# Channel mixing of a two-layer decoder trunk: all eleven pairs' early products ahead, the first operands of the downward product split before the stage border, modulation sums closed by columns

## Chip, cores and metric

The kernel runs on one core of a Trainium2 chip. The metric is the device time of one execution in microseconds (us); the median of three runs counts. One profiled execution gives the trace: PE is TensorE's matrix multiply, PEld its weight loads, DVE is VectorE, ACT ScalarE, POOL GpSimd, and SP the engine that issues nearly all DMAs, in the order of its own queue.

## What is computed

Two layers, a sequence of 1024 positions, width 1024, all float32. The part that the change touches:

```python
def reference(...):
    c_act = silu(c)
    for l in range(2):
        mod = c_act @ ada_w[l] + ada_b[l]              # 6 x 1024 modulation values
        shift_m, scale_m, gate_m, shift_f, scale_f, gate_f = split(mod, 6)
        h = rms_norm(x, g_pre_mix[l]) * (1 + scale_m) + shift_m
        ...                                            # attention beside a pooling mixer, output projection
        x = x + gate_m * rms_norm(mix, g_post_mix[l])
        h = rms_norm(x, g_pre_ffn[l]) * (1 + scale_f) + shift_f
        f = (silu(h @ w_gate[l]) * (h @ w_up[l])) @ w_down[l]     # inner width 2816
        x = x + gate_f * rms_norm(f, g_post_ffn[l])
```

## The kernel before

**Precision.** A float32 operand is split into a high part (ACT, line 213) and the rest (DVE, line 214, one subtraction), and a product is three matmuls: high by high (line 239), high by low (242), low by high (243). A split of 128x1024 is one instruction on ACT and one on DVE.

**Upward product.** The sequence is two halves of 512 positions, the inner width eleven pairs of two 128-blocks. Both products of the channel mixing use a scheme with seven block products in place of eight. For the upward product five of a pair's seven (right operands T2, T3, T1, B22, T4) need sums over both halves; two (right operands B11 and B21) need the first half alone and are the *early products*. `up_firsts` makes these for some pairs while the second half is still being normed: `FIRST = (3, 6)` says three pairs beside the attention's end and six after the output projection. Each pair there is two jobs of 24 matmuls; it stores its sums (`firsts`) and the gated result (`a11`) to DRAM. The six are interleaved with `second_norm`: four steps of the post norm, then four steps `k` (one for each 128 rows of a half) in which `up_sums` builds T1 to T4 and B22 with `split`s and sums on ACT, DVE and POOL (lines 972 to 980). `run(stream, steps, (other, n))` paces the other stream: it takes n steps of the other over `steps` steps of the stream; here 12 over 12. Then `up_pair` goes through the eleven pairs: those with early products load them back and make five products, the last two make all seven. A pair's weights stand in two `raw` tiles (two buffers); lines 1076 to 1082 form sums of weights on DVE, a `split` follows, then the matmuls.

**Downward product.** `down` makes seven products p1, p2, p5, p6, p3, p7, p4 of 11 units each (12 matmuls a unit), in groups of one, then two units. `left_of` loads a left operand from DRAM and splits it; right operands from w_down are split into tiles `bh` and `ph` or `bl`. `bh` lies in the memory of the region "down", which takes the place of the region "up" (tiles T1 to T4, B22); each tile waits until what lay there has been used. B11's rows of w_down, six transfers with 2.75 MB in all, go into the `hT` tiles, which hold the first half's B11 and B21 until the last early product has read them: `load(B11, g)` stands in the last pair's second step.

**Modulation sums.** `ada_sum` sums eight weight tiles `ar` (two buffers) times a value each on DVE (lines 271 and 273) into an `ada` tile of 128x512; summing that over partitions gives 512 values. For layer 1's first norm four such sums run beside layer 0's downward product (`ada_pair`): each is split (ACT, DVE), two matmuls against a column of ones pick it into one row of a bank (367, 368), and after the fourth the rows are copied by ACT, turned by four transposes (375) and added to the biases (379). The stream has 20 steps, and is paced 60 over 77, so that it is through after 26 units.

The order of an engine's instructions is made by a scheduler from this program, and it may put an instruction well ahead of its place in the text.

Of the kernel before, what the change touches and what calls it, by code (L numbers as in the profile page):

```python
# [12 lines left out]
F32R = mybir.dt.float32r  # L13
# [7 lines left out]
P = 128  # L21
# [44 lines left out]
def hybrid_decoder_kernel(  # L66
# [70 lines left out]
    def msc_bank():  # L137
        return ps.tile([P, 512], F32, tag="msc", name="msc", bufs=3)
# [72 lines left out]
    def split(hi, lo, src):  # L211

        nc.scalar.activation(hi, src, AF.Copy)  # L213
        nc.vector.tensor_sub(lo, src, hi.bitcast(F32))  # L214
# [44 lines left out]

    def ada_sum(l, n0, got):  # L260

        src = ada_w[l].rearrange("(p j) n -> p j n", j=KD)
        acc, ws = None, []
        for j in range(0, KD + 2, 2):
            for i, w in enumerate(ws, j - 2):
                if i == 0:
                    acc = t_("ada", [P, 512])  # L270
                    nc.vector.tensor_scalar(acc, w, c_act[:, 0:1], None, op0=ALU.mult)
                else:
                    nc.vector.scalar_tensor_tensor(  # L273
                        acc, w, c_act[:, i : i + 1], acc, op0=ALU.mult, op1=ALU.add
                    )
            ws = []
            if j < KD:
                for i in (j, j + 1):
                    w = t_("ar", [P, 512])
                    nc.sync.dma_start(w, src[:, i, n0 : n0 + 512])  # L280
                    ws.append(w)
                yield
        got += [t_("ph", [P, 512], F32R), t_("ph", [P, 512], F32R)]
        split(*got, acc)
        yield
# [73 lines left out]
    def ada_pair(l, sub, cols, ab):  # L359
# [28 lines left out]
        ]  # L388

    gates = {}  # L390

# [30 lines left out]
    def ada_stream(jobs):  # L422

        for l, n0, close in jobs:
            got = []
            yield from ada_sum(l, n0, got)
            close(*got)
# [698 lines left out]

    def down(l, wd, load, kept, fn, ended, last):

# [45 lines left out]

        def left_of(a, p0, p1, c0, c1):

            n, w = p1 - p0, c1 - c0
            raw, lh, ll = (
                part(tag, 2 * w).rearrange("p (i n) -> p i n", n=w)[:, :n, :] for tag in ("raw", "hi", "lo")
            )  # L1180
            nc.sync.dma_start(raw, kept[a][:, p0:p1, c0:c1])
            split(lh, ll, raw)
            return lh, ll

        def products(name, g, lh, ll, rights, banks, ts, evict):
# [17 lines left out]
        for name, a, right, evict in jobs[:-1]:  # L1203
            banks = [acc_bank() for _ in range(NT)]
            for g, (p0, p1) in enumerate(DOWN_GROUPS):
                n = p1 - p0
                lh, ll = left_of(a, p0, p1, 0, T)
                src = right(g)
                rights = []
                for i in range(n):  # L1210
                    rights.append((t_("bh", [P, 512], F32R), t_("ph" if count[0] % 5 < 3 else "bl", [P, 512], F32R)))
                    count[0] += 1
                    split(*rights[i], src[:, i, :])
# [12 lines left out]
        for ts in ((0, 1), (2, 3)) if last else (range(NT),):  # L1226
            banks = {t: acc_bank() for t in ts}
            for g, (p0, p1) in enumerate(DOWN_GROUPS):
                n = p1 - p0
                lh, ll = left_of(a, p0, p1, ts[0] * P, (ts[-1] + 1) * P)  # L1230
                if len(kept4) == g:
# [79 lines left out]

    FIRST = (3, 6)
    for l in range(DEPTH):
# [85 lines left out]
        if l + 1 < DEPTH:  # L1399
            nxt = layer_cols(l + 1)  # L1400
            jobs = ada_pair(l + 1, 0, nxt["cols"], nxt["abm"])
        side = ada_stream(ada_gate(l, 1))
# [14 lines left out]
        side = ada_stream(jobs)  # L1417

        region("down")
        fn = [[t_(tag, [P, D]) for _ in range(NT)] for tag in ("fn",)]  # L1420
# [21 lines left out]
        def between():  # L1442
# [15 lines left out]
        run(  # L1458
            down(l, wd, load, kept, fn, ended, not nxt), 7 * NPAIR,
            (between(), 7 * NPAIR), (side, 3 * len(jobs) * ADA),  # L1460
        )
# [39 lines left out]
```

## Time and profile before

| | |
|---|---|
| median of 3 runs | 1982.2 us (1977.94 to 1982.73) |
| the profiled execution | 1979.58 us, span of its trace 1977.8 us |
| mean granted clock of TensorE, share of full | 0.985 |
| instructions | 26045 |
| DMA | 336.62 MB, mean 170 GB/s, nearly all issued by SP |

How to read it: a matmul of 512 columns is shown as 0.39 us long, but they overlap, so the distance of their starts is what counts. A row of stretches ("windows") gives, for each, the length, the busy time and number of instructions on PE, PEld, DVE, ACT and POOL, the clock granted to TensorE (1.00 is 2.4 GHz, a mean below it is a mixture with 1.2 GHz), the mean busy share of the DMA engines, and GB/s. In a row of the order of time, [1.93 <-ACT hi L213] says that the engine stood idle for 1.93 us before this instruction and what ended the wait.

### The profile page before, as it was taken

To read this page: it belongs to the slowest core of one execution; us is meant where nothing else is said; L and a number is where in the kernel's file an instruction comes from. 1 tells how busy PE (TensorE), PEld (TensorE's weight loads), DVE (VectorE), ACT (ScalarE), POOL (GpSimd) and SP (SyncE) were. 2 spreads that over 40 slices of the span, in tenths; PEclk is the share of its full clock that TensorE was granted. 3 is DMA by queue.
4 is the path that set the end of the run, shared out by engine and by line. 5 is a ranking of instruction groups with operands and counts; after the bars stand their busy time and mean duration, and the time that the engine had idled before them with its cause. 6 is when DMAs were issued, how large, how long until landed. Compare 5 with 4: busy or idle time off the path is not lost. (4 is left out here: it accounts for less than half of the span.)

```text
span 1977.8 us, 26045 instructions
## 1 busy us (share of the span) xinstructions
PE 1891.2 (96%) x8958; PEld 1551.3 (78%) x8958; DVE 1564.9 (79%) x2907; ACT 957.1 (48%) x1794; POOL 49.7 (3%) x100
## 2 busy tenths in 40 slices
PE   6989989999999999999999899899999999999997
PEld 4877768887888887778887777788778888878886
DVE  6988976679889886787878889656788898767687
ACT  4775785653222223445648658845522222335452
POOL 1000000010000000000000000000200000000000
PEclk9999989999999999999999899899999999999999
DMA  9236553555455446842556455445555554474343
GB/s 327 88 108 187 176 192 121 160 192 192 157 180 192 161 164 229 302 129 88 178 192 182 131 146 184 135 131 189 176 192 176 175 177 170 142 262 171 112 134 112
DMA packets 222052, 336.62 MB, mean 170 GB/s; under 512 B 16696, under 2 KB 120008, under 8 KB 221920
## 3 DMA queue, kind: packets, MB, share of 16 engines
q1 hardware_dynamic: 221776, 334.92, 51.2%
q8 instruction: 70, 1.15, 0.2%
q14 instruction: 62, 0.51, 0.1%
q0 software_dynamic: 32, 0.00, 0.0%
q10 hardware_dynamic: 112, 0.04, 0.0%
HBM read 262.00 MB, written 72.89 MB: 169 GB/s over the span
## 5 line engine op out<-in xcount | busy, mean ns | idle before, releaser
L213 ACT ACTIVATE hi<-raw 128x1024 fp32r<-128x1024 f32 (+1 forms) x388 | 332.0, 867 | 335.7 <-PE acc L242 214.5
L214 DVE TENSOR_TENSOR lo<-raw,hi 128x1024 fp32r<-128x1024 f32 (+1 forms) x388 | 379.7, 984 | 80.6 <-ACT hi L213 77.1
L239 PE MATMUL acc<-t,hi 128*128 128x512 f32 x704 | 276.1, 392 | 4.9 <-ACT hi L213 4.9
L243 PE MATMUL acc<-t,lo 128*128 128x512 f32 x704 | 275.9, 393 | 3.6 <-DVE lo L214 3.6
L242 PE MATMUL acc<-t,hi 128*128 128x512 f32 x704 | 275.5, 391 | 0.0
L243 PE MATMUL acc<-bh,lo 128*128 128x512 f32 x528 | 207.1, 392 | 0.0
L239 PE MATMUL acc<-bh,hi 128*128 128x512 f32 x528 | 203.9, 391 | 3.0 <-ACT bh L213 3.0
L239 PE MATMUL acc<-hT,hi 128*128 128x512 f32 x480 | 192.0, 400 | 9.7 <-ACT hi L213 9.1
L1061 DVE TENSOR_TENSOR fn<-acc,fn 128x512 f32<-128x512 f32 x220 | 150.4, 684 | 50.9 <-PE acc L243 50.1
L242 PE MATMUL acc<-hT,hi 128*128 128x512 f32 x480 | 189.7, 395 | 0.0
L243 PE MATMUL acc<-hT,lo 128*128 128x512 f32 x480 | 187.8, 394 | 0.0
L239 PEld LDWEIGHTS acc<-t,hi 128*128 128x128 f32 x704 | 133.3, 189 | 34.1 <-ACT hi L213 6.5
L243 PEld LDWEIGHTS acc<-t,lo 128*128 128x128 f32 x704 | 133.1, 189 | 34.2 <-DVE lo L214 6.7
L242 PEld LDWEIGHTS acc<-t,hi 128*128 128x128 f32 x704 | 133.2, 189 | 27.8
L242 PE MATMUL acc<-ph,hi 128*128 128x512 f32 x320 | 126.4, 395 | 0.7 <-DVE ph L214 0.6
L239 PEld LDWEIGHTS acc<-bh,hi 128*128 128x128 f32 x528 | 99.4, 189 | 24.8 <-ACT bh L213 3.8
L273 DVE SCALAR_TENSOR_TENSOR ada<-ar,c_act,ada 128x512 f32<-128x512 f32 x140 | 104.4, 746 | 15.9 <-DMA ar<-in_ada_w_dram 14.9
L243 PEld LDWEIGHTS acc<-bh,lo 128*128 128x128 f32 x528 | 100.1, 190 | 20.7
L239 PEld LDWEIGHTS acc<-hT,hi 128*128 128x128 f32 x480 | 91.3, 190 | 29.9 <-ACT hi L213 10.8
L999 ACT ACTIVATE fn<-fn 128x512 f32<-128x512 f32 x44 | 27.8, 633 | 168.4 <-DVE fn L1061 157.9
L243 PEld LDWEIGHTS acc<-hT,lo 128*128 128x128 f32 x480 | 90.7, 189 | 18.7 <-DVE lo L214 0.4
L242 PEld LDWEIGHTS acc<-hT,hi 128*128 128x128 f32 x480 | 91.5, 191 | 17.4
(302 smaller groups left out, 3877.1 us busy)
## 6 DMA issues: line engine op xcount, KB each, us to landing
ar<-in_ada_w_dram SPq DMA_DIRECT2D x160, 256.0 KB
raw<-in_w_gate_dram SPq DMA_DIRECT2D x44, 512.0 KB
raw<-in_w_up_dram SPq DMA_DIRECT2D x44, 512.0 KB
raw<-in_w_in_dram SPq DMA_DIRECT2D x80, 256.0 KB
raw<-keeps SPq DMA_DIRECT2D x40, 512.0 KB
keeps<-fn SPq DMA_DIRECT2D x66, 256.0 KB
two_b<-in_w_down_dram SPq DMA_DIRECT2D x30, 512.0 KB
raw<-keepa SPq DMA_DIRECT2D x25, 512.0 KB
```

The costliest lines, as they stand in the source:

```text
L213: nc.scalar.activation(hi, src, AF.Copy)
L214: nc.vector.tensor_sub(lo, src, hi.bitcast(F32))
L239: ins = nc.tensor.matmul(dst, lh, rh, start=first, stop=False)
L242: nc.tensor.matmul(dst, lh, rl, start=False, stop=False)
L243: return nc.tensor.matmul(dst, ll, rh, start=False, stop=last)
L273: nc.vector.scalar_tensor_tensor(acc, w, c_act[:, i : i + 1], acc, op0=ALU.mult, op1=ALU.add)
L999: nc.scalar.activation(g, g, AF.Silu)
L1061: nc.vector.tensor_add(halves_of(dst)[m], bank, halves_of(src)[m])
```

## The change

1. `FIRST` is (3, 8): all eleven pairs make their early products ahead, and `up_pair` makes five products for each. The pacing of `second_norm` follows from the formula: 12 over 16.
2. `down_prelude`, called ahead of `region("down")`, splits the left and the right operand of the first group of p1; the right one goes into two `ph` tiles, which belong to no region.
3. Layer 1's four sums use `ada_columns`: the sum isn't split; four matmuls take a 128x128 piece of it as weights against one column of ones and give columns, which one addition joins to the biases. The stream is paced 28 over 77.

```diff
-    def ada_sum(l, n0, got):
+    def ada_sum(l, n0, got, whole=False):
...
-        got += [t_("ph", [P, 512], F32R), t_("ph", [P, 512], F32R)]
-        split(*got, acc)
+        if whole:
+            got.append(acc)
+        else:
+            got += [t_("ph", [P, 512], F32R), t_("ph", [P, 512], F32R)]
+            split(*got, acc)
         yield
...
+    def ada_columns(l, sub, cols, ab):
+        def close(r, acc):
+            bank = msc_bank()
+            for i in range(4):
+                nc.tensor.matmul(
+                    bank[:, i : i + 1], acc[:, i * P : (i + 1) * P], ones[:, 0:1], start=True, stop=True
+                )
+            m, o = r // 2, slice(r % 2 * 4, r % 2 * 4 + 4)
+            k0 = (3 * sub + 1 - m) * KD
+            nc.vector.tensor_add(ab[:, m, o], bank[:, 0:4], cols[:, k0 + o.start : k0 + o.stop])
+            if m == 0:
+                ada_scale(ab, sub, o, cols)
...
+    def down_prelude(wd, kept):
+
+        left = left_of(kept["a11"], *DOWN_GROUPS[0], 0, T)
+        right = t_("ph", [P, 512], F32R), t_("ph", [P, 512], F32R)
+        split(*right, wd[B11][0][:, 0, :])
+        return left, right
...
-                lh, ll = left_of(a, p0, p1, 0, T)
-                src = right(g)
-                rights = []
-                for i in range(n):
+                if name == "p1" and g == 0:
+                    (lh, ll), *rights = prelude
+                else:
+                    lh, ll = left_of(kept[a], p0, p1, 0, T)
+                    src = right(g)
+                    rights = []
+                for i in range(len(rights), n):
...
-    FIRST = (3, 6)
+    FIRST = (3, NPAIR - 3)
...
-            jobs = ada_pair(l + 1, 0, nxt["cols"], nxt["abm"])
+            jobs = ada_columns(l + 1, 0, nxt["cols"], nxt["abm"])
...
+        prelude = down_prelude(wd, kept)
         region("down")
...
-            down(l, wd, load, kept, fn, ended, not nxt), 7 * NPAIR,
-            (between(), 7 * NPAIR), (side, 3 * len(jobs) * ADA),
+            down(l, wd, load, kept, fn, ended, not nxt, prelude), 7 * NPAIR,
+            (between(), 7 * NPAIR), (side, 28),
```

The change moves instructions at three places. In the rows the names are those of tiles, and a row is one instruction or several alike.

**DVE, from the last norm step to the first pair, layer 0.** Lines 1076, 1077, 1081 and 1082 are the sums of the first pair's weights (now 1099, 1100, 1104, 1105), 972 and 977 the sums of the last norm step `k` = 3 (now 995 and 1000); `t_4511` (now `t_4586`) is that step's low part of T2, which the first product of a pair reads. Before:

```order
747 L1076 TENSOR_TENSOR raw<-raw 128x8x128
748 L972 TENSOR_TENSOR ar<-sa,ar 128x512
749 L214 TENSOR_TENSOR b_4535<-sa,b_4534 128x512
750 L1077 TENSOR_TENSOR raw<-raw 128x8x128
751 L214 TENSOR_TENSOR t_4519<-ar,t_4518 128x512
752 L214 TENSOR_TENSOR t_4527<-sa,t_4526 128x512
753 L977 TENSOR_TENSOR sa<-sa,ar 128x512
754 L214 TENSOR_TENSOR lo<-raw,hi 128x1024
755 L214 TENSOR_TENSOR t_4511<-sa,t_4510 128x512
```

Of the change:

```order
752 L995 TENSOR_TENSOR ar<-sa,ar 128x512
753 L214 TENSOR_TENSOR b_4610<-sa,b_4609 128x512
754 L214 TENSOR_TENSOR t_4594<-ar,t_4593 128x512
755 L214 TENSOR_TENSOR t_4602<-sa,t_4601 128x512
756 L1000 TENSOR_TENSOR sa<-sa,ar 128x512
757 L1052 TENSOR_TENSOR sb<-acc,sa 128x512
758 L214 TENSOR_TENSOR t_4586<-sa,t_4585 128x512
759 L214 TENSOR_TENSOR t_4618<-ar,t_4617 128x512
760 L1052 TENSOR_TENSOR sb<-acc,sa 128x512
761 L1099 TENSOR_TENSOR raw<-raw 128x8x128
```

The weights' sums stood in the middle of the last norm step; they now stand behind it, and two early products' additions (1052) lie between.

**SP, the same border, of the change.** The rows on `hT` are B11's loads from w_down; 1054 and 1058 store a pair's early products, 1073 and 1074 load them back, 1069 loads weights (both its rows here are the second pair's, half a pair each with its w_up twin).

```order
178 L1074 DMA sa<-keepa_3356 128x512
179 L1058 DMA keepa_3356<-sb 128x512
180 L1145 DMA hT<-in_w_down_dram 128x512
181 L280 DMA ar<-in_ada_w_dram 128x512
182 L1145 DMA hT<-in_w_down_dram 128x2x512
183 L1054 DMA firsts<-sa 128x1024
...
189 L1145 DMA hT<-in_w_down_dram 128x2x512
190 L1069 DMA raw<-in_w_gate_dram 128x4x256
191 L1069 DMA raw<-in_w_up_dram 128x4x256
...
195 L1145 DMA hT<-in_w_down_dram 128x2x512
196 L280 DMA ar<-in_ada_w_dram 128x512
197 L1069 DMA raw<-in_w_gate_dram 128x4x256
```

Before, the six `hT` loads stand at the end of the upward product, beside the last pair's stores; they now stand a whole stage earlier, four of them ahead of the second pair's weights.

**PE, where a modulation sum is closed beside layer 0's downward product.** Before, the fourth (367 and 368 are the picks); below it one of the change, 399.

```order
3516 L243 MATMUL acc<-bh,lo 128x512
3517 L239 MATMUL acc<-bh,hi 128x512 x4
3518 L367 MATMUL msc<-ph,picks 4x512
3519 L368 MATMUL msc<-ph,picks 4x512
3520 L242 MATMUL acc<-ph,hi 128x512
```

```order
3568 L243 MATMUL acc<-bh,lo 128x512
3569 L399 MATMUL msc<-ones_r,ada 128x1 x4
3570 L239 MATMUL acc<-bh,hi 128x512
3571 L242 MATMUL acc<-bl,hi 128x512
```

The picks stand in the middle of a group and read what ACT and DVE have just split; the column sums stand between two groups and read the sum itself.

## Rows read from the trace of the kernel before

**Rows 1.** The page's first part: busy time, share of the span and instructions of each engine.
```profile
PE 1891.2 (96%) x8958; PEld 1551.3 (78%) x8958; DVE 1564.9 (79%) x2907; ACT 957.1 (48%) x1794; POOL 49.7 (3%) x100
```

**Rows 2.** PE in order of time, layer 0, from the last early product to the first pair: start, us, line, what, [idle before and what ended it].
```profile
447.12 0.23 PE L300 MATMUL msc<-ident,rows 72*128 72x72 f32 x1
449.28 0.50 PE L239 MATMUL acc<-t,hi 128*128 128x512 f32 x1 [1.93 <-ACT hi L213]
...
451.13 0.73 PE L243 MATMUL acc<-t,lo 128*128 128x512 f32 x1 [1.12 <-DVE lo L214]
451.66 0.63 PE L239 MATMUL acc<-t,hi 128*128 128x512 f32 x1
```

**Rows 3.** Stretches of 5 us at the same border: length, then busy us (instructions) of PE, PEld, DVE, ACT, POOL; granted clock; DMA share; GB/s.
```profile
445.00:450.00 5.00, 3.07 (x14) 1.98 (x12) 5.00 (x7) 2.80 (x5) 1.62 (x1) 1.00 0.39 154
450.00:455.00 5.00, 3.88 (x11) 3.07 (x11) 4.86 (x5) 1.86 (x3) 2.13 (x1) 0.66 0.47 130
455.00:460.00 5.00, 4.00 (x18) 2.85 (x17) 4.96 (x9) 2.11 (x3) 0.00 (x0) 1.00 0.51 159
460.00:465.00 5.00, 4.62 (x20) 3.60 (x20) 4.96 (x7) 0.84 (x1) 0.00 (x0) 1.00 0.52 145
```

**Rows 4.** The same stretches at the same border of layer 1.
```profile
1420.00:1425.00 5.00, 4.57 (x21) 3.45 (x19) 5.00 (x6) 3.24 (x7) 1.62 (x1) 1.00 0.55 190
1425.00:1430.00 5.00, 2.31 (x6) 1.58 (x7) 5.00 (x6) 2.61 (x5) 2.14 (x1) 0.74 0.45 157
1430.00:1435.00 5.00, 5.00 (x15) 3.89 (x14) 4.85 (x8) 1.41 (x3) 0.00 (x0) 0.57 0.48 131
```

**Rows 5.** ACT, DVE and POOL in order of time, layer 0, norm steps: line 475 opens a step `k` (the first and the last of four), 975 is POOL's part of the last.
```profile
417.01 1.44 ACT L475 ACTIVATE sa<-msc,colp 128x512 f32<-128x512 f32 x2
...
442.14 1.43 ACT L475 ACTIVATE sa<-msc,colp 128x512 f32<-128x512 f32 x2
...
443.48 1.22 DVE L1076 TENSOR_TENSOR raw<-raw 128x1024 f32<-128x1024 f32 x1
...
445.81 2.32 DVE L1077 TENSOR_TENSOR raw<-raw 128x1024 f32<-128x1024 f32 x1
...
451.00 1.76 DVE L214 TENSOR_TENSOR t<-sa,t 128x512 fp32r<-128x512 f32 x1
...
445.43 1.62 POOL L975 TENSOR_TENSOR sa<-sa 128x512 f32<-128x512 f32 x1 [3.86 <-DVE ar L972]
```

**Rows 6.** Stretches of 25 us in layer 0's upward product: pairs with five products, and the last pair with seven.
```profile
600.00:625.00 25.00, 25.00 (x112) 20.54 (x111) 23.37 (x33) 7.10 (x8) 0.00 (x0) 1.00 0.65 221
...
750.00:775.00 25.00, 25.00 (x112) 20.69 (x111) 15.41 (x21) 5.57 (x7) 0.00 (x0) 1.00 0.42 148
```

**Rows 7.** PE in order of time, an undisturbed stretch: two matmuls of line 239 with two others between them.
```profile
600.10 0.39 PE L239 MATMUL acc<-t,hi 128*128 128x512 f32 x1
...
600.78 0.39 PE L239 MATMUL acc<-t,hi 128*128 128x512 f32 x1
```

**Rows 8.** PE and ACT in order of time, at the border to the downward product: layer 0 (first three rows) and layer 1.
```profile
778.25 1.19 PE L239 MATMUL acc<-bh,hi 128*128 128x512 f32 x4 [1.49 <-ACT bh L213]
...
776.62 1.06 ACT L213 ACTIVATE hi<-raw 128x1024 fp32r<-128x1024 f32 x1 [0.77 <-PE acc L242]
777.58 2.70 ACT L213 ACTIVATE bh<-hT 128x512 fp32r<-128x512 f32 x5
...
1756.38 1.19 PE L239 MATMUL acc<-bh,hi 128*128 128x512 f32 x4 [1.49 <-ACT bh L213]
```

**Rows 9.** PE in order of time, layer 0's downward product: the picks of the third and of the fourth modulation sum.
```profile
813.83 0.39 PE L367 MATMUL msc<-ph,picks 128*4 128x512 f32 x1 [0.86 <-ACT ph L213]
814.91 0.39 PE L368 MATMUL msc<-ph,picks 128*4 128x512 f32 x1 [0.69 <-DVE ph L214]
...
854.59 0.39 PE L367 MATMUL msc<-ph,picks 128*4 128x512 f32 x1 [1.27 <-ACT ph L213]
856.27 0.39 PE L368 MATMUL msc<-ph,picks 128*4 128x512 f32 x1 [1.29 <-DVE ph L214]
```

**Rows 10.** Stretches of 5 us around these two places.
```profile
810.00:815.00 5.00, 3.45 (x16) 2.28 (x14) 5.00 (x8) 3.18 (x6) 0.00 (x0) 1.00 0.92 317
815.00:820.00 5.00, 4.79 (x14) 3.52 (x14) 4.99 (x7) 0.25 (x1) 0.00 (x0) 0.66 0.94 329
...
850.00:855.00 5.00, 3.71 (x16) 2.51 (x14) 5.00 (x7) 2.73 (x4) 0.00 (x0) 1.00 0.67 215
855.00:860.00 5.00, 3.52 (x9) 2.54 (x10) 4.75 (x7) 0.59 (x1) 0.00 (x0) 0.74 0.13 47
```

**Rows 11.** PE in order of time: four column sums of the kernel's opening (two instructions each, the same form as line 399's), and the four transposes of a modulation row.
```profile
53.44 0.95 PE L344 MATMUL msc<-ones_r,ar 128*128 128x1 f32 x8
...
863.24 0.41 PE L375 MATMUL msc<-ident,ar 4*128 4x4 f32 x4
```

**Rows 12.** SP and DVE in order of time, layer 0: the issue of the second half of the first pair's weights and of the second pair's, and the first sum over the latter.
```profile
436.10 0.43 SPq L1046 DMA_DIRECT2D raw<-in_w_gate_dram  x1
...
467.83 0.38 SPq L1046 DMA_DIRECT2D raw<-in_w_gate_dram  x1
...
473.35 1.23 DVE L1076 TENSOR_TENSOR raw<-raw 128x1024 f32<-128x1024 f32 x1 [0.54 <-issue]
```

More of the change, by code (lines that the diff above doesn't have):

```diff
@@ L388, in ada_pair @@
         ]
+    def ada_columns(l, sub, cols, ab):
[10 more added lines that the diff above has]
+                ada_scale(ab, sub, o, cols)
+        return [
+            (l, (3 * sub + 1 - r // 2) * D + r % 2 * 512, lambda acc, r=r: close(r, acc), True)
+            for r in range(4)
+        ]
     gates = {}
@@ L422, in ada_stream @@
     def ada_stream(jobs):
-        for l, n0, close in jobs:
+        for l, n0, close, *whole in jobs:
             got = []
-            yield from ada_sum(l, n0, got)
+            yield from ada_sum(l, n0, got, *whole)
             close(*got)
@@ L1125, in down_loads, with left_of, down @@
         return wd, load
-    def down(l, wd, load, kept, fn, ended, last):
+    def left_of(a, p0, p1, c0, c1):
+        n, w = p1 - p0, c1 - c0
+        raw, lh, ll = (
+            part(tag, 2 * w).rearrange("p (i n) -> p i n", n=w)[:, :n, :] for tag in ("raw", "hi", "lo")
+        )
+        nc.sync.dma_start(raw, a[:, p0:p1, c0:c1])
+        split(lh, ll, raw)
+        return lh, ll
+    def down_prelude(wd, kept):
[3 more added lines that the diff above has]
+        return left, right
+    def down(l, wd, load, kept, fn, ended, last, prelude):
         (c11, c12), (c21, c22) = [[[c[:, i * 512 : (i + 1) * 512] for c in fn[h]] for i in range(2)] for h in range(2)]
@@ L1173, in down @@
         right4 = combine(b21, b21, b12)
[L1175 to L1183, printed above, removed]
         def products(name, g, lh, ll, rights, banks, ts, evict):
@@ L1229, in down @@
                 n = p1 - p0
-                lh, ll = left_of(a, p0, p1, ts[0] * P, (ts[-1] + 1) * P)
+                lh, ll = left_of(kept[a], p0, p1, ts[0] * P, (ts[-1] + 1) * P)
                 if len(kept4) == g:
```

## The prediction

> **What bounds the kernel now.** I read the busy shares first, then PE's waits, then stretches of 5 us around each, and last the order of time on ACT, DVE, POOL and SP there. PE is busy for 96% of the span [rows 1]; matmuls of 512 columns start 0.227 us apart when nothing disturbs them (three in 0.68 us [rows 7]). So time can be won only where PE stands still or runs below full clock. The change touches three such places.
>
> At the border from the early products to the first pair, PE waits 1.93 us for the pair's first high part and soon after 1.12 us for its low part [rows 2]; DVE is busy without a gap meanwhile [rows 3]. The granted clock, 1.00 until then, falls to a mean of 0.66 in the 5 us after the wait: for part of them TensorE is at 1.2 GHz, and its matmuls stand as 0.63 us instead of 0.39 [rows 2, 3]. Layer 1 has the same [rows 4]. At the border to the downward product PE waits 1.49 us in either layer for the first `bh` [rows 8]. And beside layer 0's downward product it waits twice for the two parts of a modulation sum that have just been split [rows 9], with DVE again full and the clock at 0.66 and 0.74 behind it [rows 10].
>
> **Part 1, all eleven pairs early.** Two pairs' two early products move ahead in each layer: 2 x 2 x 24 matmuls x 0.227 = 21.8 us of PE work changes its place, none is added. What it buys is cover. The norm steps form a chain: the first opens at 417.01, the last at 442.14, and the last low part of T2 is done at 451.00 + 1.76 = 452.76 [rows 5], 35.8 us in all. PE reached the border at 447.12 + 0.23 = 447.35 [rows 2], so the chain was 5.4 us late. With 12 steps paced over 16, step 7, which opens the chain, comes after job 9 of 16 instead of job 7 of 12: seven jobs (38.1 us) follow it instead of five (27.2), 10.9 us more. The chain should then be through 5.5 us before the border. DVE's sums of weights no longer stand in its middle, so the 2.32 us of line 1077, beside POOL's 975 [rows 5], leaves it too.
>
> What is late next is the first pair's own operand: the second half of its weights is issued 11.2 us ahead of the border [rows 2, 12], and its `raw` tile is freed by the last early operand, so that distance stays. Behind it come two sums of 1.22 us (2.32 where POOL works beside it) and a split of 1.06, as now. I leave 1.0 us a layer for it. Its bounds are 0 and the whole of today's wait.
>
> What there is to win, from the stretches: layer 0, idle 1.93 + 1.12 + 1.00 + 0.38 = 4.4 us and clock (1 - 0.66) x 5 = 1.7, together 6.1 [rows 3]; layer 1, idle 0.43 + 2.69 = 3.1 and clock (0.26 + 0.43) x 5 = 3.5, together 6.6 [rows 4]. Less twice 1.0: **10.7 us**. The Trainium skill, "TensorE: Matmul & The Clock Gate", section "Part 1: The HAM clock gate", says that the slow clock is the default and activity releases it, so that any closed gap should also return clock. The rows at the downward border differ, 1.49 us idle without a slow matmul behind it [rows 8], and I count clock only where a stretch shows it.
>
> In the upward product the last two pairs lose their seven-product ease. DVE goes from 15.4 of 25 us there to the 23.4 that pairs with five products show; PE stood at 25.0 of 25 beside that [rows 6], so it costs nothing. If DVE fell behind, PE would wait for each pair's remainder. Added transfers are 2.25 MB for each moved pair (1 MB of weights again, 0.5 out, 0.75 back), 9.4 million bytes in all, 29 us at the 329 GB/s of [rows 10]; DMA is at a share of 0.39 to 0.65 in the stretches that they go into [rows 3, 6], so they are hidden. Uncovered they would cost these 29 us. SP also issues 28 more DMAs at some 0.4 us [rows 12], none of which a busy engine needs soon.
>
> **Part 2, the prelude.** The 1.49 us come from ACT: at 776.62 it splits a later left operand, which had waited for the last upward matmul, and only then `bh` [rows 8]. With the first group's right operand in `ph`, split long before, PE goes on at once for 12 x 0.227 = 2.7 us. Meanwhile ACT does the same 0.96 us and then two `bh` of 0.54 (2.70 over five [rows 8]), 2.0 in all; DVE's second low part (some 0.6 us) needs a `ph` tile that the first group frees only at its end, and PE needs that part four matmuls, 0.9 us, later; I leave 0.2 us for it, an estimate. Gain 2 x (1.49 - 0.2) = **2.6 us**, bounds 0 and 3.0.
>
> **Part 3, column sums.** Removed are 8 picks x 0.227 = 1.8 us and four transposes, 0.41 [rows 11]; added are four times 0.95 us of column sums [rows 11], 3.8: 1.6 us more on PE. The waits go: a sum's last DVE instruction now stands at least a group (5.4 us of PE) ahead of its close, because the stream takes less than one step in a group of two units, and neither ACT nor DVE splits it. They were worth idle 1.55 + 0.21 and clock 1.7 at the one place, idle 1.29 + 1.48 and clock 1.3 at the other, 7.5 us [rows 10]. DVE's 32 instructions for the sums now last over 55 units instead of 26 and meet busier stretches of p6 and p3; I leave 0.6 us for that. Gain 7.5 - 1.6 - 0.6 = **5.3 us**, bounds -1.6 and 5.9. The first norm piece of the next layer needs the last column at step 61, and its close comes at step 56, so nothing follows from the later end.
>
> **Sum.** 10.7 + 2.6 + 5.3 = 18.6 us off the profiled execution's 1979.6, 1961.0; the median of the runs stands 2.6 above that execution, so I forecast **1963.6 us**. Bounds of the terms: up to 3.0 more (the two unresolved waits at zero, DVE's allowance unused), and some us more if undercounted clock comes back; up to 8 less for each part that keeps its wait.
>
> **Rivals.**
> *The border keeps its wait* (12%). The first pair's operand, not the norm chain, was the true limit: the first wait in [rows 2] names its high part, not T2. For it: that row. Against it: DVE and ACT were behind because of the norm steps [rows 5]. Then some 4 us a layer stay, 1971.6.
> *The sums' waits move* (10%). DVE is full at both places [rows 10] with other work too; if the spread sums only fill it elsewhere, part 3 costs its 1.6 us and wins nothing: 1970.5. Both together (9%), 1978.5, would be no change: 0.3% is 6 us, about what a measurement of this kernel can tell.
> *The w_down transfers stand in the way, and it is slower* (7%). The six `hT` loads, 2.75 MB or 2.9 million bytes, 8.8 us at 329 GB/s, are issued at the border now, on the queue that the first two pairs' weights use. The second pair's second half was issued at 467.83 and used at 473.35 with DVE idle before it [rows 12], so there is little slack. If they hold up the first pair's second half or the second pair by all 8.8 us, a layer loses 8.8, 1.7 of clock, and the 5.4 that part 1 would have won: 15.9, twice 31.7, 1995.3. It decides from about 12 us a layer against my forecast. Against it: four of the six wait for an early product of the last pair, and by then the first pair's second half has been issued for nearly 6 us; only one more stands ahead of the second pair's second half. The Trainium skill, "DMA: Bandwidth & Descriptors", section "Queues, rings and completion order", says that descriptors are consumed in ring order on each DMA engine, so what SP issues first would go first. That rule is this rival's; no row here shows by itself how two queued transfers share.
>
> **Chances.** Forecast 62%, the first two rivals 22%, both 9%, slower 7%: faster 0.84, same 0.09, slower 0.07. The range for 8 in 10 goes from 1952 (the bounds above) to 1975, past either single rival.
>
> **What would show it.** Right: after the last early product PE goes on within 1 to 2 us at both layers and the clock stays at 1.00; no wait for `bh` at the downward border; no PE wait near the four column sums, 0.95 us each; the pairs at 25.0 of 25 on PE. Wrong: a wait for `hi` or DMA in the first two pairs, DVE at 5.0 of 5 with PE gaps in p5 to p3, or a new wait on `ph` at the first group's end over 1 us.

## The result and the profile after

The changed kernel takes 1962.72 us (median of four runs, 1960.9 to 1966.43) beside 1981.39 us (four runs, 1977.94 to 1982.73) of the kernel before on the same chip: a ratio of 0.9911, 95% interval 0.9891 to 0.993. The forecast was 1963.6 us in 1952 to 1975. The number came out, but not by the sum that led to it: its largest term is nearly missing, and two others are larger than forecast.

The first part of the page after, which answers to [rows 1]. The traced span is 16.6 us shorter (1961.2 for 1977.8); PE's busy time falls by 5.7 of them, though it runs 20 instructions more, and the other 10.9 were idle time.

```profile
PE 1885.5 (96%) x8978; PEld 1551.6 (79%) x8978; DVE 1561.8 (80%) x2906; ACT 953.6 (49%) x1789; POOL 48.8 (2%) x100
```

The ends of the stages show where the time went. PE in order of time, before: last early product, last matmul of layer 0's upward and downward product, last early product and last upward matmul of layer 1.

```profile
446.89 0.39 PE L243 MATMUL acc<-hT,lo 128*128 128x512 f32 x1
...
776.37 0.39 PE L243 MATMUL acc<-t,lo 128*128 128x512 f32 x1
...
1004.06 0.39 PE L243 MATMUL acc<-two_b,lo 128*128 128x512 f32 x1
...
1424.18 0.39 PE L243 MATMUL acc<-hT,lo 128*128 128x512 f32 x1
...
1754.50 0.39 PE L243 MATMUL acc<-t,lo 128*128 128x512 f32 x1
```

The same matmuls after, and the first of the downward product behind the second row:

```profile
467.21 0.39 PE L243 MATMUL acc<-hT,lo 128*128 128x512 f32 x1
...
776.02 0.39 PE L243 MATMUL acc<-t,lo 128*128 128x512 f32 x1
776.24 0.39 PE L239 MATMUL acc<-ph,hi 128*128 128x512 f32 x1
...
993.46 0.39 PE L243 MATMUL acc<-two_b,lo 128*128 128x512 f32 x1
...
1432.91 0.39 PE L243 MATMUL acc<-hT,lo 128*128 128x512 f32 x1
...
1739.61 0.39 PE L243 MATMUL acc<-t,lo 128*128 128x512 f32 x1
```

In each layer 96 matmuls, 96 x 0.227 = 21.8 us, have moved from the upward product into the early ones. With them put back, layer 0's upward product takes 308.8 + 21.8 = 330.6 us (308.8 from 467.21 to 776.02) where it took 329.5: it lost 1.1. Layer 1's takes 328.5 for 330.3, a gain of 1.8. The two borders to the downward product win 1.65 each (0.22 us from matmul to matmul, as anywhere, for 1.88), layer 0's downward product, from its own first matmul to its last, 8.6 (217.2 for 225.8). The rest, 1.5 up to the end of layer 0's early products and 2.5 from layer 1's start to the end of its own, lies where I had expected nothing.

**The border of part 1.** PE after the last early product and 30 us later, in the second pair, of layer 0 (compare [rows 2]), and the stretches there and in layer 1's second pair (compare [rows 3, 4]):

```profile
468.97 0.50 PE L239 MATMUL acc<-t,hi 128*128 128x512 f32 x1 [1.31 <-ACT hi L213]
...
470.55 0.50 PE L243 MATMUL acc<-t,lo 128*128 128x512 f32 x1 [0.84 <-DVE lo L214]
...
498.32 0.50 PE L239 MATMUL acc<-t,hi 128*128 128x512 f32 x1 [0.73 <-ACT hi L213]
...
500.58 0.79 PE L243 MATMUL acc<-t,lo 128*128 128x512 f32 x1 [1.52 <-DVE lo L214]
```

```profile
465.00:470.00 5.00, 3.40 (x15) 2.26 (x13) 5.00 (x6) 1.54 (x2) 0.00 (x0) 1.00 0.62 215
470.00:475.00 5.00, 4.45 (x20) 3.68 (x20) 5.00 (x7) 2.54 (x3) 0.00 (x0) 1.00 0.87 302
495.00:500.00 5.00, 3.33 (x14) 2.12 (x12) 5.00 (x7) 1.69 (x2) 0.00 (x0) 1.00 0.31 108
500.00:505.00 5.00, 4.42 (x13) 3.60 (x14) 5.00 (x8) 0.85 (x2) 0.00 (x0) 0.66 0.48 168
...
1460.00:1465.00 5.00, 3.88 (x16) 2.56 (x15) 5.00 (x7) 1.70 (x2) 0.00 (x0) 1.00 0.91 312
1465.00:1470.00 5.00, 4.58 (x13) 3.63 (x14) 5.00 (x8) 1.01 (x2) 0.00 (x0) 0.66 0.49 177
```

The border still costs 2.15 us of waiting, and the second pair, where layer 0 had no wait before, costs 2.25 us and 1.7 of clock. DVE and SP between the two places say why:

```profile
461.35 0.69 DVE L214 TENSOR_TENSOR t<-ar,t 128x512 fp32r<-128x512 f32 x1 [0.15 <-ACT t L213]
...
464.87 1.23 DVE L1099 TENSOR_TENSOR raw<-raw 128x1024 f32<-128x1024 f32 x1 [2.22 <-DMA ar<-in_ada_w_dram]
...
486.41 0.75 DVE L273 SCALAR_TENSOR_TENSOR ada<-ar,c_act,ada 128x512 f32<-128x512 f32 x1 [4.80 <-DMA ar<-in_ada_w_dram]
...
494.10 1.23 DVE L1099 TENSOR_TENSOR raw<-raw 128x1024 f32<-128x1024 f32 x1 [0.28 <-issue]
```

```profile
455.18 0.41 SPq L1069 DMA_DIRECT2D raw<-in_w_gate_dram  x1
...
476.65 0.43 SPq L1145 DMA_DIRECT2D hT<-in_w_down_dram  x1
477.26 0.41 SPq L1069 DMA_DIRECT2D raw<-in_w_gate_dram  x1
...
478.52 0.56 SPq L280 DMA_DIRECT2D ar<-in_ada_w_dram  x1
...
488.92 0.38 SPq L1069 DMA_DIRECT2D raw<-in_w_gate_dram  x1
```

The norm chain's last low part ends at 461.35 + 0.69 = 462.04, well ahead of the border. Then DVE stands idle for 2.22 us until the second half of the first pair's weights, issued from 455.18 on, has landed. The row names `ar`, but line 1099 reads `raw` alone: by the trace's semaphores the last of these weights lands at 464.68, and in e10 below, where no load of the gate sum is in flight, the same wait is put down to `raw`. And at 481.6 DVE stops for 4.80 us at one instruction of the gate sum (the modulation sum that runs beside the upward product). Its load `ar`, issued at 478.52 behind w_down transfers and the first half of the second pair's weights, lands at 486.31. The low part that follows on DVE waits too: ACT had its high part done by 482.15, and it starts at 487.68. So `raw` comes free late, and the second pair's second half is issued at 488.92, its first sum made at 494.10.

That is 25.1 us after the first pair's first matmul; before it was 24.1 (473.35 - 449.28, [rows 2, 12]). One us alone makes no stall. But before, PE reached the second pair only 32.3 us after that matmul, since the first pair's own waits and slow clock held it up. PE of the kernel before, at the second pair's first matmul:

```profile
481.60 0.39 PE L239 MATMUL acc<-t,hi 128*128 128x512 f32 x1
```

Now it is there after 28.6 (498.32 - 0.73 - 468.97). DVE's first sum stood 8.2 us ahead of PE's need and stands 3.5 ahead: the waits that part 1 took away had been the second pair's cover.

**Parts 2 and 3.** The downward product starts at 776.24 with `ph`, without a wait [rows 8]. The column sums have no wait ahead of them and no slow matmul behind, and the stretches that stood at 3.45 and 3.52 of 5 [rows 10] are full. PE at the first of them, and the two stretches:

```profile
814.42 0.95 PE L399 MATMUL msc<-ones_r,ada 128*128 128x1 f32 x8
815.23 0.49 PE L239 MATMUL acc<-bh,hi 128*128 128x512 f32 x1
815.55 0.40 PE L242 MATMUL acc<-bl,hi 128*128 128x512 f32 x1
```

```profile
810.00:815.00 5.00, 5.00 (x27) 4.22 (x26) 2.23 (x3) 1.59 (x4) 0.00 (x0) 1.00 0.96 339
...
855.00:860.00 5.00, 5.00 (x27) 4.24 (x26) 4.86 (x10) 1.15 (x2) 0.00 (x0) 1.00 0.70 248
```

### The profile page after: what moved, and what is told of

Its sections match the earlier page's. It is cut to its first block, busy times and chain, and to the rows that moved or that the text cites. A ratio compares the mean times of both kernels' runs of the same rounds, so it can differ in the third digit from the quotient of the medians.

```text
span 1961.2 us, 26137 instructions
## 1 busy us (share of the span) xinstructions
PE 1885.5 (96%) x8978; PEld 1551.6 (79%) x8978; DVE 1561.8 (80%) x2906; ACT 953.6 (49%) x1789; POOL 48.8 (2%) x100
## 4 chain that ended last, share of the span: by engine, by line
PE 76%; DVE 11%; DMA 6%; ACT 4%; issue 2%; SPq 0%; POOL 0%; DVEq 0%; ACTq 0%; POOLq 0%
PE acc L243 23%; PE acc L239 23%; PE acc L242 23%; DMA ar<-in_ada_w_dram 3%; DVE lo L214 2%; PE msc L839 1%; DMA raw<-in_w_up_dram 1%; DVE ada L273 1%; ACT raw L498 1%; PE pv L239 1%; DMA ar<-x 1%; PE pv L242 1%; ACT hi L213 1%; PE pv L243 1%; DVE t L214 1%
## 5 line engine op out<-in xcount | busy, mean ns | idle before, releaser
L213 ACT ACTIVATE hi<-raw 128x1024 fp32r<-128x1024 f32 (+1 forms) x388 | 331.9, 867 | 335.1 <-PE acc L242 200.4
L243 PE MATMUL acc<-bh,lo 128*128 128x512 f32 x520 | 202.4, 389 | 0.0
```

Of the source, the lines that this page charges most:

```text
L243: return nc.tensor.matmul(dst, ll, rh, start=False, stop=last)
```

## The experiments

All in one table: the ratio to the kernel before, and from each trace the time between the matmuls that end the stages, in us, with moved early products put back (21.8 us; 10.9 for ten pairs) so that the columns compare. The downward product is counted from its own first matmul, so the border ahead of it stands in no column. The expectations below give upward products as they stand in the trace, without the 21.8 us. Layer 1's downward product lies between 209.5 and 211.2 everywhere.

| kernel | ratio (95%) | to last early, 0 | upward 0 | downward 0 | to last early, 1 | upward 1 |
|---|---|---|---|---|---|---|
| before | 1 | 446.9 | 329.5 | 225.8 | 420.1 | 330.3 |
| the change | 0.9911 (0.9891 to 0.993) | 445.4 | 330.6 | 217.2 | 417.7 | 328.5 |
| e11, the change again | 0.9917 (0.9901 to 0.9932) | 445.4 | 329.5 | 217.2 | 418.8 | 328.4 |
| e1, part 1 alone | 0.9978 (0.9965 to 0.999) | 446.5 | 330.0 | 226.2 | 419.7 | 328.3 |
| e2, part 2 alone | 0.996 (0.9944 to 0.9976) | 447.0 | 329.7 | 222.2 | 418.6 | 329.7 |
| e3, part 3 alone | 0.9954 (0.9939 to 0.9969) | 446.8 | 329.7 | 216.3 | 417.9 | 331.9 |
| e12, parts 2 and 3 | 0.9935 (0.992 to 0.995) | 445.9 | 330.4 | 217.2 | 417.5 | 332.9 |
| e7, picks at the slow pace | 0.9963 (0.9948 to 0.9978) | 444.4 | 331.0 | 220.0 | 419.7 | 331.6 |
| e4, w_down held | 0.991 (0.9895 to 0.9926) | 446.7 | 327.7 | 217.2 | 418.5 | 327.5 |
| e5, gate sum held | 0.9893 (0.9875 to 0.9911) | 445.4 | 326.3 | 217.8 | 417.5 | 330.5 |
| e6, both held | 0.9903 (0.9884 to 0.9922) | 446.1 | 330.4 | 217.5 | 417.7 | 330.8 |
| e8, ten pairs, w_down held | 0.9948 (0.9931 to 0.9966) | 445.8 | 331.5 | 217.2 | 418.3 | 329.8 |
| e9, w_down and first sums held | 0.9933 (0.992 to 0.9947) | 448.4 | 330.4 | 217.2 | 418.8 | 330.0 |
| e10, all three held | 0.991 (0.9896 to 0.9925) | 448.9 | 327.0 | 217.2 | 418.6 | 328.2 |

The theory at the outset: part 1's gain is given back at the second pair by transfers in SP's queue, and parts 2 and 3 carry the result. The rival: the terms of the prediction, 10.7, 2.6 and 5.3.

### The parts alone: e1, e2, e3, e12

The first three are the kernel before with one part each; e12 is the change with

```diff
-    FIRST = (3, NPAIR - 3)
+    FIRST = (3, 6)
```

> The kernel before with part 1 alone: all eleven pairs make their early products ahead; no prelude, and the modulation sums are closed by picks as before. Theory (from the profile after): the wait at the border shrinks, but its price comes back at the second pair, because the w_down transfers now stand among the weights and the gate sum's transfers in SP's queue; part 1 wins 1 to 5 us of the 1981.4, so 1976 to 1980, and the trace shows PE waits of over 1 us at the second pair's first product in both layers. Rival (the prediction's own term): part 1 wins 10.7 us, 1970.7, and nothing stands in the second pair. If it is over 1981.4, part 1 costs more than it wins.

> The kernel before with part 2 alone: the first operands of the downward product are split ahead of the stage border. Theory: the 1.49 us at each of the two borders go, with nothing given back: 2.6 to 3.3 us off 1981.4, so 1978.1 to 1978.8. Rival: with FIRST at (3, 6) the first B11 transfer lands only in the last pair, so the split of its first operand is late and the wait stays: 1981.4, and the trace shows a wait at the first matmul of the downward product.

> The kernel before with part 3 alone: the four modulation sums beside layer 0's downward product are closed by columns and paced 28 over 77. Theory (from the profile after, by the time from the first to the last matmul of that product, 225.8 us before and 217.2 after): 8.6 us, so 1972.8. Rival (the prediction's own term): 5.3 us, 1976.1. Second rival: the stream's sums disturb DVE elsewhere when parts 1 and 2 are absent: over 1978.

> The change without its part 1: FIRST stays at (3, 6), parts 2 and 3 as changed. Theory (part 1 is worth 2 to 5 us, as it was alone): 0.993 to 0.9945 of the kernel before, with the border's waits of before and a downward product of 217 us in layer 0. Rival (the prediction's term of 10.7 us holds in company): 0.996 to 0.997. Second rival (part 1 is worth nothing beside the other two): 0.991 to 0.992, as the whole change.

**e1**: 1974.44 us for 1978.6, by the ratio 4.4 us less (2.0 to 6.9), as the theory had it and less than half of the term. Its second pair waits too, in other portions than expected: 0.63 and, at 507.94, 1.03 us in layer 0, 0.98 and 1.03 in layer 1.

**e12** says the same from the other side: without part 1 the ratio is 0.9935, with it 0.9911 and 0.9917, so in company it would be worth 0.0018 to 0.0024, about 4 us; but the intervals of e12 and of the change overlap, so only e1 shows that it is more than nothing. The border's first wait is that of before:

```profile
448.27 0.50 PE L239 MATMUL acc<-t,hi 128*128 128x512 f32 x1 [1.96 <-ACT hi L213]
```

**e3**: 1969.81 us, by the ratio 9.1 us less (6.1 to 12.1). Its downward product of 216.3 us agrees with the theory's 8.6 and more; the interval leaves 6.1 open, not 5.3.

**e2** is a miss of both theories: 1970.36 us, by the ratio 7.9 us less (4.7 to 11.1), where 2.6 to 3.3 had been expected. The borders win their 1.65 each, but the downward product behind them also takes 3.6 us less. The prelude takes one unit's split out of it and so shifts by one unit which units use the `ph` tiles, and the picks stand elsewhere than in [rows 9]. None of them waits in e2; the largest wait of that product is this one, three matmuls behind the last picks, and the clock stays at 1.00 after it:

```profile
858.78 0.50 PE L242 MATMUL acc<-ph,hi 128*128 128x512 f32 x1 [1.78 <-DVE ph L214]
```

Part 3 removes these picks, so parts 2 and 3 win the same 3.6 us only once: 4.4 + 7.9 + 9.1 = 21.4 us alone, and 16.4 to 17.6 together; parts 2 and 3 make 7.9 + 9.1 - 3.6 = 13.4, and e12 has 12.9. Why the order of ACT's and DVE's work suits the picks better there was not tried.

### Was it the column form or the pace: e7

The kernel before with its splits and picks, and one line changed:

```diff
-            (between(), 7 * NPAIR), (side, 3 * len(jobs) * ADA),
+            (between(), 7 * NPAIR), (side, 28),
```

> The kernel before, with the four modulation sums still closed by splits and picks, but paced 28 over 77 as in the change. Theory (the split in the middle of the group makes the wait, whatever the pace): the picks' waits move to other places of the downward product and stay, 225 us for layer 0's downward product, 0.998 to 1.001 of the kernel before. Rival (the pace was it: DVE gets more time for each sum): the waits go, 217 to 219 us there, 0.996.

1973.61 us for 1979.6, and 220.0 us in the downward product, one above the rival's 217 to 219: the expectation fell, and its rival holds in the main. [rows 9] calls the picks at 813.83 the third sum's; they are the second's, after those at 797.42. In e7 the picks nearest to that place, lines 370 and 371, are the first sum's, and they follow each other without a wait:

```profile
815.63 0.40 PE L370 MATMUL msc<-ph,picks 128*4 128x512 f32 x1
815.87 0.40 PE L371 MATMUL msc<-ph,picks 128*4 128x512 f32 x1
```

So of part 3's 8.6 us some 5.8 are the slower pace. The other 2.8 aren't lost at the picks: none of e7's waits, and around its four sums PE loses no more than at the change's columns. Some 2.2 of them lie where the next layer's norm begins, where e7's PE waits 1.41 us for ACT (at 973.61) and the change's doesn't. Whether the form causes that was not tried, so no part of the gain is shown to be the form's. A split in the middle of a group need not be late; it was late at a pace at which DVE was full there (5.00 of 5 [rows 10]).

### What holds up the second pair: e4, e5, e6

e4 orders each w_down load into `hT` on SP's queue behind the weights of pair 8 (of 0 to 10); e5 does the like with the gate sum's loads, behind the weights of the pair whose step issues them, from pair 4 on, and lets that stream begin ten steps later; e6 does both. `after` sets only the order on the engine. The main lines of e4's edit:

```diff
-            nc.sync.dma_start(w, rows[odd][:, p0:p1, dh * 512 : (dh + 1) * 512])
+            ins = nc.sync.dma_start(w, rows[odd][:, p0:p1, dh * 512 : (dh + 1) * 512])
+            if name == B11:
+                after(ins, issued[8])
```

> The changed kernel, with the six w_down transfers into the hT tiles held on SP's queue behind the weights of pair 8 of the upward product, so that they no longer stand at the border. Theory: they delay the second pair's weights and the gate sum's transfers (DVE idle 4.8 us for them), and the second pair's stall of about 4 us a layer comes from that; without them it goes: 1962.7 less 6 to 8, so 1955 to 1957, and PE shows no wait over 0.5 us in the second pair. Rival: the second pair is late because its raw tiles are freed late, transfers or not: the stall stays and the time is within 2 us of 1962.7. Second rival: held back, they collide with the last pairs' weights: a new wait there and over 1963.

> The changed kernel, with the gate sum's transfers (the ada_w loads beside the upward product) held on SP's queue until pair 4's weights have been issued; the w_down transfers stay at the border. Theory: DVE, which works in order, stood idle 4.8 us for one of these loads behind the w_down transfers, and that made the second pair's operands late; without the loads the second pair's stall goes although the w_down transfers stay: 6 us less in the two upward products (from 308.8 and 306.7 us to 305 to 306 each), 0.988 of the kernel before. Rival: the w_down transfers themselves delay the second pair's weights by 5 us: the stall stays, 0.991.

> The changed kernel with both held: the w_down transfers behind pair 8's weights and the gate sum's behind pair 4's. Theory (the border's rest is the first pair's own weights, issued 9 us ahead into DMA engines that already move 390 GB/s): the 1.0 to 1.6 and 0.84 us of waits at the border stay, the second pair has no wait at all, and the last pairs' low part (1.0 us at 753) too, since DVE is eased at neither place: 0.988 of the kernel before, upward products 304 to 306 us. Rival: the gate sum's loads and DVE's sums were the border's rest: the border's waits fall below 0.5 us and the upward products to 303 us, 0.986.

**e4**: layer 0's second pair has no wait left, and its upward product takes 2.9 us less than the change's, layer 1's 1.0 less. DVE still waits for `ar`, but 2.08 us, and its first sum stands 6.2 us ahead of PE's arrival. The two stretches of the stall, DVE, and PE's first matmul of the second pair:

```profile
495.00:500.00 5.00, 5.00 (x23) 4.13 (x22) 4.97 (x7) 1.70 (x2) 0.00 (x0) 1.00 0.01 3
500.00:505.00 5.00, 5.00 (x24) 4.13 (x22) 5.00 (x8) 2.65 (x3) 0.00 (x0) 1.00 0.31 120
```

```profile
484.65 1.54 DVE L273 SCALAR_TENSOR_TENSOR ada<-ar,c_act,ada 128x512 f32<-128x512 f32 x2 [2.08 <-DMA ar<-in_ada_w_dram]
...
493.81 1.23 DVE L1103 TENSOR_TENSOR raw<-raw 128x1024 f32<-128x1024 f32 x1 [1.26 <-issue]
...
1449.80 1.54 DVE L273 SCALAR_TENSOR_TENSOR ada<-ar,c_act,ada 128x512 f32<-128x512 f32 x2 [3.24 <-DMA ar<-in_ada_w_dram]
```

```profile
500.01 0.39 PE L239 MATMUL acc<-t,hi 128*128 128x512 f32 x1
```

The whole time doesn't show it: 0.991 is the ratio of the change, and the upward products win 3.9 us in the traces, not the 6 to 8 expected. In layer 1 the w_down transfers are the smaller part: DVE waits 3.24 us for `ar` without them (last row) and 4.04 with them, in the change at 1451.29, since the load stands behind the second pair's own weights as well. PE's second pair keeps a wait of 1.04 us there, as it had 1.03 before.

**e5** leaves the w_down transfers at the border and takes the gate sum away from it. Layer 0's second pair is clean there too: its first sum, at 488.82, stands 8.5 us ahead of PE at 497.37, and the upward product has its least value, 326.3. With the gate sum held, PE has no wait in the second pair in either layer, here as in e6 and in e10 below. With the w_down transfers alone held that isn't so: besides layer 1 of e4, the second pair of e9 below waits 1.03 us in each layer. So what the stall needs is the instruction on DVE that waits for its load in the queue; the w_down transfers ahead of that load lengthen the wait, from 2.08 to 4.80 us in layer 0 and from 3.24 to 4.04 in layer 1. The gate sum isn't free where it has gone: PE waits 1.03 us in layer 0's seventh pair and 0.88 and 1.71 in layer 1's seventh and ninth, the last behind a DVE wait of 1.86 us for `ar`. So of the two upward products, 304.5 and 308.7 us in the trace, the second misses the 305 to 306 expected.

```profile
488.82 1.23 DVE L1106 TENSOR_TENSOR raw<-raw 128x1024 f32<-128x1024 f32 x1 [0.25 <-DMA raw<-in_w_up_dram]
...
1646.93 0.75 DVE L275 SCALAR_TENSOR_TENSOR ada<-ar,c_act,ada 128x512 f32<-128x512 f32 x1 [1.86 <-DMA ar<-in_ada_w_dram]
```

```profile
497.37 0.39 PE L239 MATMUL acc<-t,hi 128*128 128x512 f32 x1
...
1655.40 0.50 PE L243 MATMUL acc<-t,lo 128*128 128x512 f32 x1 [1.71 <-DVE lo L214]
```

**e6** misses its 304 to 306: its traced upward products have waits of up to 1.03 us in later pairs. Its traced execution was 6.9 us above its own median, so these numbers are not its usual ones. Of these, e5 has the lowest ratio, but its interval and that of the change overlap: none is shown to beat it.

### What is left of the border: e8, e9, e10, e11

e8 is e4 with `FIRST = (3, NPAIR - 4)`. e9 is e4 with the first pair's loads of early sums held behind the store of pair 9's gated result; e10 is e9 with the gate sum's loads behind pair 1's weights, its stream five steps later. The main lines of e9's edit:

```diff
+            if p == 0:
+                for ins in loads:
+                    after(ins, stored[NPAIR - 2])
```

> The changed kernel with FIRST at (3, 7), ten pairs early, and the w_down transfers held behind pair 8's weights. One pair less to cover the norm chain: six jobs follow step 7 where the change has seven, so the chain has 5.4 us less. Theory (the chain has 5 us to spare at eleven pairs, and the border's rest is the weights' landing): the border's waits stay at 2 us a layer, the wait in the last pair at 753 goes with its seven-product ease, and the time is within 2 us of eleven pairs held: 0.989 to 0.991. Rival: the chain is late again, the border's waits rise to 3 us with a fall of the clock: 0.992 to 0.994.

> The changed kernel with the w_down transfers held behind pair 8's weights, and the first pair's two loads of early sums (768 KB) held behind the store of the last early pair but one, so that they no longer share the DMA engines with the first pair's weights. Theory (the border's rest is these weights, which land 9 to 10 us after their issue while the DMA engines move 390 GB/s): they land about 2 us earlier, DVE's idle time before the first pair's first sum (2.2 us in the change) goes, and the border's waits (2.2 us in layer 0, 2.1 in layer 1) fall below 1 us a layer; 2 to 4 us less than with the w_down transfers held alone, 0.989 of the kernel before. Rival: each DMA engine takes descriptors in the order of their issue, so what is issued later took nothing from the weights: the border stays as it is, 0.991.

> As the one before, with the gate sum's transfers held too, behind pair 1's weights. Theory: at the border nothing but the first pair's weights is in flight, and DVE has no sum for the gate between that pair's operands: both of the border's waits go below 0.5 us, and the gate sum runs in the pairs 1 to 4 without a PE wait, since DVE has 1.6 us to spare in 25: upward products 303 to 305 us in both layers, 0.987 to 0.988 of the kernel before. Rival: the gate sum's 16 DVE instructions make PE wait wherever they go, as they did behind pair 4: upward products 306 to 309 us, 0.990.

> The change itself once more, beside the two others on the same chip. By the first four runs 0.991 of the kernel before; upward products 308.8 and 306.7 us, with the second pair's waits of 0.7 and 1.5 us in layer 0 and 1.5 in layer 1. If these waits are missing here, they are chance of one execution and not of the change.

**e8**: the rival holds in the main: 0.9948, a little above its 0.992 to 0.994 (interval 0.9931 to 0.9966). DVE ends the norm chain at 455.41 + 0.69 and goes on without a gap to the first pair's sums, whose weights had landed by 454.42, and PE, which reached the border at 457.1, waits 3.12 us. At ten pairs DVE's chain is the limit, at eleven the landing of the weights.

```profile
455.41 0.69 DVE L214 TENSOR_TENSOR t<-ar,t 128x512 fp32r<-128x512 f32 x1
...
456.62 1.22 DVE L1103 TENSOR_TENSOR raw<-raw 128x1024 f32<-128x1024 f32 x1
```

```profile
460.25 0.50 PE L239 MATMUL acc<-t,hi 128*128 128x512 f32 x1 [3.12 <-ACT hi L213]
```

**e9** and **e10**: the theory falls. In e10, with nothing issued behind the weights until 469.88, DVE waits for them nearly as in the change, 1.93 us for 2.22 (2.01 in e9), and they take 9.2 us from issue to first use where the change takes 9.7 (455.18 to 464.87):

```profile
458.81 0.45 SPq L1076 DMA_DIRECT2D raw<-in_w_gate_dram  x1
...
469.88 0.34 SPq L1064 DMA_DIRECT2D keepa<-sb  x1
```

```profile
468.02 1.23 DVE L1110 TENSOR_TENSOR raw<-raw 128x1024 f32<-128x1024 f32 x1 [1.93 <-DMA raw<-in_w_up_dram]
```

What was issued later took hardly anything from what was issued first. That agrees with the Trainium skill, "DMA: Bandwidth & Descriptors", section "Queues, rings and completion order": each DMA engine consumes descriptors in ring order. Right ahead of these weights stand the w_up part of the pair's first half and a store of early sums, issued at 454.11 and 454.63 in the change. By the trace's semaphores these land at 460.70 and 461.96, and the second half behind them at 463.26 and 464.68, in the order of issue. Before, the two halves were issued 10.1 us apart (425.98 and 436.10), now 3.3 (451.93 and 455.18), and the last transfer lands 9.0 us after its issue where it took 6.1. An earlier release of `raw` was not tried; so the border's last 2 us are located, not removed. e10's waits at the border, 1.59 us in layer 0 and 1.28 in layer 1, are somewhat shorter than the change's 2.15 and 2.09 but each of the two waits stays above the 0.5 expected, and where its gate sum now runs PE waits too: 1.81 us in layer 1's eighth pair. Its upward products, 305.2 and 306.4 us in the trace, lie between theory and rival. e9 is slower than e10 (0.9933 and 0.991); that was not followed up.

**e11**: the second pair's waits are there again, 1.11 and 1.03 us in layer 0, 0.35 and 1.03 in layer 1, but without a fall of the clock (1.00 in both pairs), and the upward products are 1.1 and 0.1 us shorter than in the first trace. So the 1.7 us of clock that each second pair lost in the first trace belong to that execution.

## Why the prediction came out as it did

**Part 1, 10.7 us forecast.** The first step was right: I had the chain through 5.5 us before the border, and it is (462.04, PE through at 467.44 + 0.23). The next failed, the one on "what is late next". I kept the distance from the issue of the first pair's weights to the border, 11.2 us, and left 1.0 us a layer; the trace has 2.15 and 2.09. The distance was even kept (455.18 to 467.67, 12.5 us), but the weights take 9.7 us to their first use where [rows 12] has 436.10 to a first sum at 443.48 [rows 5], 7.4: the pair's first half and a store now stand right ahead of them in the queue. The third failure is a missing term: DVE's wait for the gate sum's load, which the six transfers lengthen. I had the transfers as a rival, all or nothing, with 7%. The loss came, smaller, and by a way that the rival didn't name: through that wait for a load of another stream, and because the second pair had lost the cover of the first pair's waits. The text says "there is little slack"; in fact there were 8.2 us, of which the change itself used up 3.7 by making PE faster.

The stretches then close the account. Layer 0: 6.1 - 2.15 - 3.95 (second pair) - 1.01 (a wait at 754.79 in the last pair, where the seven-product ease is gone) = -1.0; the ends of the stages say -1.1. Layer 1: 6.6 - 2.09 - 3.24 in the second pair, which had cost 1.02 before, = 2.3; the stages say 1.8. So 0.7 us in place of 10.7 in the two upward products of that trace, 1.9 in the other trace of the change (e11). By the runs part 1 is worth some 4 us (2.0 to 6.9 in e1); beside parts 2 and 3 the traces have it in layer 1's upward product, 328.5 us for 332.9 in e12, one execution each.

**Seven-product ease "costs nothing".** Nearly: one wait of 1.01 us in one layer, 0.18 in the other execution.

**Part 2, 2.6 us.** Right in its mechanism: 1.65 a border, 3.3 in all, a little over the upper bound of 3.0; the 0.2 us for the second low part weren't needed. What e2 won beside that I hadn't seen.

**Part 3, 5.3 us.** The mechanism held, the size was off: 8.6. By the starts of its matmuls, less 0.227 us for each, PE lost 4.0 us from 811.90 to 819.96 and 5.0 from 852.25 to 860.86, 9.0 in all, where I read 7.5 from stretches of 5 us; two smaller waits of 0.4, at 797.9 and 956.2, I hadn't counted; a column sum costs 0.90 (1.36 us from the matmul before it, at 814.19, to the second behind it, at 815.55, less two at 0.227) and not 0.95; and DVE's 0.6 wasn't needed. Of the rivals, the first was half right: behind the norm chain the first pair's operand is the limit, at 2 us a layer and not at 4. The second was wrong, the sums' waits moved nowhere. Of the two reasons that the term names for the waits to go, the slower stream and the missing split, e7 shows the first alone to be worth 5.8 us.

**The sum.** Part 1 is 10.0 short; parts 2 and 3 give 4.0 more than forecast; 4.0 came from stretches without a term, the opening and layer 1's start. The opening differs between kernels that are equal there: the table's first column runs from 444.4 to 448.9, and I count its 1.5 as what one execution differs from another. For layer 1's start that isn't shown: the column there has 418.6 to 420.1 in the four kernels with picks and 417.5 to 418.8 in the ten with column sums, so a part of the 2.5 may be part 3's. The terms then make 18.6 - 10.0 + 4.0 + 4.0 = 16.6 us, the difference of the two traces. So the number was right to 0.9 us by terms that cancel, and that is luck.

## What to carry to other kernels

A wait that is removed was cover for what follows: measure how far ahead of the engine's arrival the next operand stands, and take the removed wait from that. Where transfers are let free earlier, ask which instruction on an in-order engine waits for a load issued behind them; that engine hands the wait on to work that has nothing to do with either. And before replacing a form, try its pace: 5.8 of 8.6 us came from spreading the same splits, and none of the rest is shown to be the form's.

## What the runs showed of the hardware

TensorE's granted clock is not told by the size of the gaps ahead of it. In the first trace of the change waits of 1.31 and 0.84 us in a row left it at 1.00. In the second trace of the same kernel 0.96 and 0.84 us at the same place were followed by a mean of 0.66 over 5 us, so that TensorE was at 1.2 GHz for part of them, which costs (1 - 0.66) x 5 = 1.7 us:

```profile
468.56 0.50 PE L239 MATMUL acc<-t,hi 128*128 128x512 f32 x1 [0.96 <-ACT hi L213]
...
470.14 0.80 PE L243 MATMUL acc<-t,lo 128*128 128x512 f32 x1 [0.84 <-DVE lo L214]
```

```profile
470.00:475.00 5.00, 4.86 (x15) 3.87 (x16) 5.00 (x8) 2.53 (x3) 0.00 (x0) 0.66 0.83 288
```

So a clock term read from one execution is worth something between zero and what it shows. And a load can hold up DVE for 4.80 us although DVE's busy share is 80%: the wait comes from where the load stands in SP's queue, not from how much DVE has to do.
